# Strassen down-projection of a decoder layer: all 22 row blocks, a third weight buffer, splits moved into the up-projection and parked in HBM

## The chip, the cores and the metric

The kernel runs on one core of one Trainium2 chip. The metric is the device time of one execution in microseconds (us). Before the change three runs took 729.5, 730.12 and 730.3 us; the median is 730.12 us. The profile was taken in a further execution, which took 731.23 us.

## What is computed

One layer of a decoder trunk: a modulated RMSNorm, an input projection into two groups of heads (a gated linear recurrence and sparse attention), an output projection, and then a gated MLP. There are T = 512 tokens and D = 1024 model columns; all arrays are f32. The change lies in the last step, the MLP, cut here to what matters:

```python
h2 = rmsnorm(x, norm2_g[l]) * (1.0 + sc2) + sh2            # 512 x 1024
u = causal_dwconv(h2 @ w_up[l], conv_w[l], conv_b[l])      # 512 x 5632, conv of width 3
a, v = jnp.split(u, 2, axis=-1)
x = x + gt2 * ((jax.nn.silu(a) * v) @ w_down[l])           # (512 x 2816) @ (2816 x 1024)
```

## The kernel before

Matmuls run on fp32r operands. To keep f32 accuracy every operand is held as two fp32r parts: `hi`, a cast of the f32 value on ScalarE (`split`, L140 to L142), and `lo`, the f32 value less `hi`, a subtraction on VectorE. A product of two such operands takes three matmuls (`mm3`, L145 to L147). All work is issued from Python in one fixed order, and each engine runs its own instructions in that order. So an instruction that waits holds up everything behind it on its engine.

**Weights.** `load`, `issue` and `take` (L169, L202, L212) keep two f32 weight tiles, tag `raw`, in SBUF: `take(i)` hands out tile i and issues the load of tile i+1 on SyncE's queue (SP). `parts` splits a tile of 128 x 1024 into `whi` and `wlo`; each of these tags has two buffers. A form, below, is such a pair. The pair that is being consumed by TensorE and the pair that is being made are the two.

**The up stage.** There are 44 steps, two for each of the 22 blocks f of 128 hidden columns (128 rows of `w_down`): step 2f makes the block of `a`, step 2f+1 that of `v`. `up_mm(st)` (L1567) issues the 24 matmuls of a step into one PSUM bank and, ahead of them, the split of the weights of step st+1. `up_post` (L1577), two steps behind, applies the convolution: an ACTIVATE on ScalarE (L1582), two SCALAR_TENSOR_TENSOR on VectorE (L1583, L1584), then for `a` the silu on ScalarE (L1587), for `v` the product with it on GpSimd (L1589). `g_parts` (L1598) then takes the finished block y (128 x 512): it splits what the down stage needs at once, and forms Strassen sums of token halves on GpSimd (L1617 to L1620), which stay in f32. `ada_last` (L1361), one step for each up step as long as it has any (20 of them), computes the vector gt2 on GpSimd from weights that it streams through a tile with tag `aw`.

**The down stage.** The 512 x 2816 by 2816 x 1024 product is done by Strassen's scheme with seven products in place of eight (Winograd's sums), over halves of the tokens, halves of the columns, and pairs of neighbouring row blocks (even, odd). Before, it covers the first 20 of the 22 blocks: ten pairs, taken two at a time in NQ = 5 groups q. The last two blocks are multiplied in the plain way (`plain`, L1794). The four PSUM accumulators, two banks each, are called r, w, s, v. One group of one product is 12 matmuls of 128 x 512 columns: two pairs, two token blocks, three matmuls.

The weight sums are made on the fly: `prep_a` yields the forms b11 and b12-b11, `prep_b` b21 and a sum kept in `keep`, `prep_c` b22 and b22-b12, `prep_d` the two plain blocks and then the kept sums. Each sum is one VectorE TENSOR_TENSOR of 128 x 1024 (L1680, L1685, L1691, L1698). `s_parts` (L1666) splits the f32 token sums `gS` into `gH`, 20 times, between the forms. `ahead_of` (L1743) makes one form ahead of the one in use.

Where Strassen's scheme uses a partial sum in two outputs, the bank is copied out (`taken_snap`, L1732, ScalarE; L1779, VectorE) and folded into the residual rows `rest` on GpSimd (`rest_add`, L1737, with L1740 and L1741), while the bank goes on accumulating. `dn_out` (L1803) multiplies a bank by gt2, adds `rest` (L1806, L1807, VectorE) and stores the result.

SBUF tiles of 4 KB per partition come from one pool, `gran`, of 35 buffers (`G`).

## Time and profile before

| what | value |
|---|---|
| median of three runs | 730.12 us |
| the profiled execution: its time | 731.23 us |
| its span, first to last instruction | 729.1 us |
| mean granted TensorE clock over the span | 0.986 |
| PE busy | 690.1 us, 95% of the span |
| VectorE (DVE) busy | 534.7 us, 73% |
| ScalarE (ACT) busy | 352.7 us, 48% |
| GpSimd (POOL) busy | 190.1 us, 26% |
| moved by DMA | 99.63 MB, 137 GB/s over the span |

The matmuls of the up stage (tile `u`) start between 332.5 and 577.4 us, those of the down stage (tile `dn`) between 580.6 and 725.0 us. Matmuls are pipelined: a row of a 128 x 512 matmul shows about 0.39 us, while the next starts about 0.23 us later. So waits are read from the distance of the starts and from the view of waits, not from the busy time. In the views a row names the engine, the line, the operation, what it writes and reads, and in brackets the idle time of its engine ahead of it with the instruction that ended it. PEclk is the granted TensorE clock, 1.00 being full.

### The profile page before, as it was taken

Reading aid. Unit: us, or ns where it says so; the run is one execution under the profiler, and the core shown is the slowest. Engines: PE = TensorE matmul, PEld = TensorE weight load, DVE = VectorE, ACT = ScalarE, POOL = GpSimd, SP = SyncE. Lnnn points to the kernel's source line nnn. Section 1 sums busy time; section 2 is a strip of 40 time slices with the busy share of each in tenths; the row PEclk is TensorE's granted clock in tenths of the full one; section 3 lists DMA queues with packets and bytes.
Section 4 is the critical chain, followed back from the end, with each engine's and each line's share of the span. In section 5 each row is a group of like instructions: output and inputs, shape, how many; then the busy total and the mean of one; then the engine's idle time right before and its main releaser. Section 6 shows DMA issues by size and latency. Waiting matters only on the chain.

```text
span 729.1 us, 10084 instructions
## 1 busy us (share of the span) xinstructions
PE 690.1 (95%) x3752; PEld 564.2 (77%) x3752; DVE 534.7 (73%) x960; ACT 352.7 (48%) x661; POOL 190.1 (26%) x175
## 2 busy tenths in 40 slices
PE   8999999999999999999999999999999888879857
PEld 4678888688888888889888877788888666658645
DVE  5688989998998986877566656666656557898553
ACT  5554448546777774346433524434343345344311
POOL 1007243330000002000397378332321301230300
PEclk9999999999999999999999999999999989999998
DMA  9997542682321234443535264244243136454220
GB/s 290 284 267 241 174 147 88 195 254 74 116 70 70 69 113 174 118 125 111 157 103 146 82 179 131 72 116 113 65 112 116 58 118 234 167 173 148 83 84 31
DMA packets 101444, 99.63 MB, mean 137 GB/s; under 512 B 5979, under 2 KB 83603, under 8 KB 101397
## 3 DMA queue, kind: packets, MB, share of 16 engines
q1 hardware_dynamic: 100565, 96.80, 43.3%
q10 hardware_dynamic: 832, 2.20, 0.8%
q8 instruction: 29, 0.48, 0.3%
q14 instruction: 18, 0.15, 0.1%
HBM read 94.79 MB, written 4.20 MB: 136 GB/s over the span
## 4 chain that ended last, share of the span: by engine, by line
PE 55%; DVE 24%; ACT 7%; issue 4%; SPq 4%; POOL 3%; DMA 2%; ACTq 0%; POOLq 0%; DVEq 0%
DVE wlo L142 9%; PE u L146 6%; PE u L147 6%; PE u L145 6%; ACT whi L141 4%; PE dn L146 3%; PE dn L147 3%; PE dn L145 3%; PE oT L1050 3%; PE pT L145 2%; PE pT L147 2%; PE pT L146 2%; SPq L282 2%; PE F L1022 2%; DVE y L1584 2%
## 5 line engine op out<-in xcount | busy, mean ns | idle before, releaser
L142 DVE TENSOR_TENSOR wlo<-raw,whi 128x1024 fp32r<-128x1024 f32 (+1 forms) x87 | 118.6, 1364 | 61.2 <-ACT whi L141 60.5
L147 PE MATMUL u<-h2h,wlo 128*128 128x512 f32 (+1 forms) x360 | 137.1, 381 | 1.9 <-DVE wlo L142 1.9
L145 PE MATMUL u<-h2h,whi 128*128 128x512 f32 (+1 forms) x360 | 136.9, 380 | 0.0
L146 PE MATMUL u<-h2l,whi 128*128 128x512 f32 (+1 forms) x360 | 136.8, 380 | 0.0
L141 ACT CAST whi<-raw 128x1024 fp32r<-128x1024 f32 (+1 forms) x87 | 89.5, 1029 | 48.4 <-PE dn L147 24.0
L147 PEld LDWEIGHTS u<-h2h,wlo 128*128 128x128 f32 x360 | 67.7, 188 | 15.9 <-DVE wlo L142 3.2
L146 PEld LDWEIGHTS u<-h2l,whi 128*128 128x128 f32 x360 | 67.7, 188 | 12.8
L145 PEld LDWEIGHTS u<-h2h,whi 128*128 128x128 f32 x360 | 67.7, 188 | 12.7
L1589 POOL TENSOR_TENSOR y<-y,y 128x512 f32<-128x512 f32 x22 | 28.4, 1289 | 130.2 <-DVE y L1584 130.2
L358 POOL TENSOR_TENSOR hrs<-hrs,mhalf 128x4 f32<-128x4 f32 (+2 forms) x16 | 20.1, 1266 | 136.8 <-DVE hrs L357 136.7
L990 ACT ACTIVATE pt<-pt,mx 128x128 f32<-128x128 f32 (+3 forms) x64 | 35.8, 562 | 20.0 <-DVE mx L974 19.7
L1587 ACT ACTIVATE y<-y 128x512 f32<-128x512 f32 x22 | 13.9, 632 | 55.1 <-DVE y L1584 55.1
L141 ACT CAST whi<-keep 128x1024 fp32r<-128x1024 f32 x15 | 15.6, 1049 | 49.8 <-PE dn L147 28.7
L146 PE MATMUL dn<-wlo,gH 128*128 128x512 f32 x80 | 32.7, 409 | 6.9 <-DVE wlo L142 6.9
L145 PE MATMUL pT<-hT,whi 128*128 128x512 f32 x96 | 38.8, 404 | 0.0
L147 PE MATMUL pT<-hT,wlo 128*128 128x512 f32 x96 | 37.6, 392 | 0.0
L146 PE MATMUL pT<-hT,whi 128*128 128x512 f32 x96 | 37.6, 391 | 0.0
L142 DVE TENSOR_TENSOR wlo<-keep,whi 128x1024 fp32r<-128x1024 f32 x15 | 19.0, 1274 | 25.2 <-ACT whi L141 25.1
L146 PE MATMUL dn<-wlo,gT 128*128 128x512 f32 (+1 forms) x58 | 24.6, 425 | 12.5 <-DVE wlo L142 12.5
L1584 DVE SCALAR_TENSOR_TENSOR y<-u,cv,y 128x510 f32<-128x510 f32 x44 | 32.9, 748 | 1.6
L1582 ACT ACTIVATE y<-u,cv 128x512 f32<-128x512 f32 x44 | 33.9, 772 | 0.0
L1583 DVE SCALAR_TENSOR_TENSOR y<-u,cv,y 128x511 f32<-128x511 f32 x44 | 32.6, 741 | 1.4 <-ACT y L1582 1.4
(362 smaller groups left out, 1673.4 us busy)
## 6 DMA issues: line engine op xcount, KB each, us to landing
raw<-in_w_up SPq DMA_DIRECT2D x44, 512.0 KB, 5.2
raw<-in_w_down SPq DMA_DIRECT2D x16, 1024.0 KB, 4.7
aw<-in_w_ada SPq DMA_DIRECT2D x24, 512.0 KB, 4.1
ada<-in_w_ada SPq DMA_DIRECT2D x32, 256.0 KB, 5.8
raw<-in_w_in SPq DMA_DIRECT2D x7, 1024.0 KB, 6.4
x<-in_x SPq DMA_DIRECT2D x8, 512.0 KB, 5.2
raw<-in_w_cmp SPq DMA_DIRECT2D x8, 512.0 KB, 5.1
raw<-in_w_out SPq DMA_DIRECT2D x4, 1024.0 KB, 5.8
```

What stands on the lines that cost most here:

```text
L141: sc.copy(hi, src)
L142: (eng or ve).tensor_tensor(lo, src, f32(hi), ALU.subtract)
L145: pe.matmul(o, ah, bh, start=start, stop=False, skip_group_check=True)
L146: pe.matmul(o, ah, bl, start=False, stop=False, skip_group_check=True)
L147: pe.matmul(o, al, bh, start=False, stop=stop, skip_group_check=True)
L358: gp.tensor_tensor(o, o, mhalf[:, 0:n], ALU.pow)
L990: sc.activation(pt[:, sl], pt[:, sl], AF.Exp, bias=mx[:, e:e + 1], scale=-1.0, accum_out=su[:, h % 2, e:e + 1])
L1050: pe.matmul(oTs[i][r:r + 64, h // 2], VV[:, j, b, g], src[:, q * P:(q + 1) * P], start=(h == 0 and b == 0 and j == 0), stop=False, skip_gr ...
L1582: sc.activation(y, u, AF.Identity, bias=cv[:, 132 + c:133 + c], scale=cv[:, 88 + c:89 + c])
L1583: ve.scalar_tensor_tensor(y[:, 1:], u[:, :T - 1], cv[:, 44 + c:45 + c], y[:, 1:], ALU.mult, ALU.add)
L1584: ve.scalar_tensor_tensor(y[:, 2:], u[:, :T - 2], cv[:, c:c + 1], y[:, 2:], ALU.mult, ALU.add)
L1589: gp.tensor_tensor(ys[0], ys[0], y, ALU.mult)
```

## The change

Six things change, all in the MLP.

1. **All 22 blocks go through Strassen.** NJ becomes 11 pairs, in NQ = 6 groups; the last group has one pair. The plain part goes. The groups are taken in the order SEQ = 0 0 1 1 2 2 3 3 4 5 4 5, the first mention of a group being its first product of a pass, the second its other product. Tiles of half size take their f32 weights from `gran` (`rawd`).
2. **A third weight buffer, two forms ahead.** `form` puts every third form into a tile `w3`, which takes the room of tag `aw` (free once `ada_last` is done). Two calls of `look` ahead of the down stage, and one in each `get`, keep two forms ahead of the one in use. The first two are issued ahead of the last but one `up_post`.
3. **Token sums are split in the up stage.** `g_parts` only notes what is to be split (`pend`); `park`, at the head of the next `up_post`, issues the splits. So the split of the last pair falls into the first pass of the down stage.
4. **Parts that are used late are parked in HBM.** The splits `st22` (256 columns) and `st34` (512) of each pair are written out by ScalarE's queue one `up_post` after that, 22 stores, and read back by SP in the down stage: 11 loads `S34` of 512 KB, 6 loads `A22`, 5 of 512 KB and one of 256 KB.
5. **Banks are seeded instead of folds.** A partial sum that goes into a second output is put into that output's bank, ahead of its products: by ScalarE (`end_a`, bank to bank), by VectorE (`end_b`, `end_c`, with the SBUF copy w5). GpSimd's folds go. Outputs are finished by `dn_out` as their banks complete, two in the third pass and four in the fourth.
6. **`ada_last` takes two steps in every three** (`if st % 3`).

The lines of the changed kernel lie 1 to 6 lines lower in the unchanged parts (L142 becomes L143, L1582 becomes L1588).

```diff
-NJ = 10
-NQ = NJ // 2
+NJ = NFF // 2
+NQ = NJ // 2 + 1
+SEQ = [q for q in range(NQ - 2) for _ in range(2)] + [NQ - 2, NQ - 1] * 2
...
+            if name[0] == "d" and shape[0] * shape[1] <= 1024:
+                raw = G(shape, s="rawd")
+            else:
+                raw = wp.tile([P] + shape, F32, tag="raw", name=nm("raw"))
...
         u = us.pop(st)
+        park()
...
+    def park():
+
+        while parked:
+            sc.dma_start(*parked.pop(0))
+        while pend:
+            split(*pend.pop(0))
+        parked.extend(parking)
+        parking.clear()
...
         if not odd:
-            if b == 0:
-                A1[j // 2] = G([2, 2, 256], F32R, s="gA")
-            split(A1[j // 2][:, b, 0], A1[j // 2][:, b, 1], y[:, h1])
+            gP[j] = G([2, 2, 256], F32R, s="gP")
+            pend.append((gP[j][:, 0, 0], gP[j][:, 0, 1], y[:, h1]))
...
+        pend.extend([(gQ[j][:, 0, 0], gQ[j][:, 0, 1], y[:, h1]), (st22[:, 0], st22[:, 1], y[:, h2]),
+                     (gP[j][:, 1, 0], gP[j][:, 1, 1], s12[:, 0]), (gQ[j][:, 1, 0], gQ[j][:, 1, 1], s12[:, 1]),
+                     (st34[:, 0], st34[:, 1], s34)])
+        parking.extend([(pk22[:, j], f32(st22)), (pk34[:, j], f32(st34))])
...
-        next(ada2, None)
+        if st % 3:
+            next(ada2, None)
...
+    def form(src):
+
+        made[0] += 1
+        if made[0] % 3 != 2:
+            return parts(src)
+        t = wp.tile([P, 2] + list(src.shape)[1:], F32R, tag="aw", name=nm("w3"), bufs=1)
+        split(t[:, 0], t[:, 1], src)
+        return t[:, 0], t[:, 1]
...
     def prep_b(q):
         raw = take(f"db{q}")
-        ve.tensor_tensor(keep[q], raw[:, :, 512:D], keep[q], ALU.subtract)
-        b21 = parts(raw[:, :, 0:512]) if q < NQ - 1 else None
-        if b21:
-            yield b21
-        s_parts(1, q)
-        yield parts(keep[q])
-        ve.tensor_tensor(keep[q], raw[:, :, 0:512], keep[q], ALU.subtract)
-        if not b21:
-            yield parts(raw[:, :, 0:512])
+        b21, b22 = raw[:, :, 0:512], raw[:, :, 512:D]
+        ve.tensor_tensor(keep[q], b22, keep[q], ALU.subtract)
+        yield form(keep[q])
+        yield form(b21)
+        ve.tensor_tensor(keep[q], b21, keep[q], ALU.subtract)
...
+    def phase(xb, x, yb, y, start=False, done=None, each=None):
+        seen = set()
+        for n, q in enumerate(SEQ):
+            w = get()
+            if q not in seen:
+                seen.add(q)
+                product(xb, x, q, w, start)
+                if each:
+                    each(q)
+                if q == NQ - 1:
+                    done()
+            else:
+                product(yb, y, q, w, start)
+
+    def end_a():
+        for a in range(2):
+            sc.copy(bS[a], bR[a])
+
+    def end_b():
+        for a in range(2):
+            ve.tensor_tensor(bV[a], bR[a], w5[a], ALU.add)
...
+    phase(bR, 1, bW, 5, True, end_a, each_a)
+    w5 = [TMP([P, T], tag="w5") for _ in range(2)]
+    for a in range(2):
+        sc.copy(w5[a], bW[a])
+    phase(bR, 6, bS, 2, False, end_b, each_b)
+    phase(bR, 7, bV, 3, False, end_c, each_c)
+    outs = [(bV[0], 0, 1), (bV[1], 1, 1), (bW[0], 2, 1), (bW[1], 3, 1)]
+    ws = []
+    for q in range(NQ):
+        w = get()
+        if q < NQ - 2:
+            product(bR, 4, q, w)
+            dn_out(*outs[q])
+        else:
+            ws += [(hi[:, b], lo[:, b], 2 * q + b) for hi, lo in [w] for b in range(min(2, NJ - 2 * q))]
+    for a, cols in ((0, slice(0, 512)), (1, slice(0, 256)), (1, slice(256, 512))):
+        for n, (hi, lo, j) in enumerate(ws):
+            mm3(bR[a][:, cols], *stat(4, j, a), hi[:, cols], lo[:, cols], False, n == len(ws) - 1)
+        dn_out(bR[a], 2 + a, 0, cols.start, cols.stop)
```

The order of the instructions shows what moved. In the **up stage on ScalarE**, over the four steps of one pair of blocks, before (`gA` and `gT` are the splits of a finished block, `whi` the weights of the next step, `u` a step's PSUM bank):

```order
L1587 ACTIVATE y_5109<-y_5109 128x512
L141 CAST whi_5118<-raw_5041 128x1024
L1582 ACTIVATE y_5146<-u_5040,cv 128x512
L141 CAST gT_5151<-y_5109 128x512
L141 CAST whi_5161<-raw_5041 128x1024
L1582 ACTIVATE y_5189<-u_5080,cv 128x512
L1587 ACTIVATE y_5189<-y_5189 128x512
L141 CAST whi_5198<-raw_5115 128x1024
L1582 ACTIVATE y_5226<-u_5114,cv 128x512
L141 CAST gA_5077<-y_5189 128x256
```

and after the change, the same place in the four steps (`gP`, `gQ` stay in SBUF, the `st` tiles are parked):

```order
L142 CAST whi_5533<-raw_5454 128x1024
L1588 ACTIVATE y_5561<-u_5453,cv 128x512
L142 CAST whi_5576<-raw_5454 128x1024
L142 CAST gQ_5572<-y_5524 128x256
L142 CAST st_997_5573<-y_5524 128x256
L142 CAST gP_5492<-s_994_5566 128x256
L142 CAST gQ_5572<-s_994_5566 128x256
L142 CAST st_998_5574<-s_995_5567 128x512
L1588 ACTIVATE y_5614<-u_5493,cv 128x512
L1593 ACTIVATE y_5614<-y_5614 128x512
L142 CAST whi_5623<-raw_5530 128x1024
L1611 DMA pk_3608<-st_997_5573 128x512
```

The splits now stand behind the next step's `whi`, in one group of five for an odd block, and the two stores follow one step later, in front of the next L1588.

In the **second pass of the down stage on VectorE** (two groups; `keep` the kept weight sum), before:

```order
L1691 TENSOR_TENSOR keep_5696<-raw_5843,keep_5696 128x1024
L1685 TENSOR_TENSOR keep_5747<-raw_5886,keep_5747 128x1024
L142 TENSOR_TENSOR wlo_5943<-raw_5886,whi_5942 128x1024
L142 TENSOR_TENSOR gH_5962<-gS_4510,gH_5962 128x2x256
L142 TENSOR_TENSOR wlo_5966<-keep_5747,whi_5965 128x1024
L1691 TENSOR_TENSOR keep_5747<-raw_5886,keep_5747 128x1024
```

and after (`w` is the third buffer, `wlo` the other two):

```order
L1708 TENSOR_TENSOR keep_5845<-raw_6050,keep_5845 128x1024
L1705 TENSOR_TENSOR keep_5895<-raw_6083,keep_5895 128x1024
L143 TENSOR_TENSOR w_1094_6124<-keep_5895,w_1094_6124 128x1024
L143 TENSOR_TENSOR wlo_6142<-raw_6083,whi_6141 128x1024
L1708 TENSOR_TENSOR keep_5895<-raw_6083,keep_5895 128x1024
```

The `gH` subtraction has gone from between the forms, and the form of the kept sum comes first.

At the **end of the second pass on VectorE**, before:

```order
L1691 TENSOR_TENSOR keep_5864<-raw_6021,keep_5864 128x1024
L142 TENSOR_TENSOR wlo_6084<-raw_6021,whi_6083 128x1024
L1779 TENSOR_TENSOR snap_5905<-dn_5702,snap_5905 128x512
L1779 TENSOR_TENSOR snap_5907<-dn_5706,snap_5907 128x512
L1698 TENSOR_TENSOR raw_6060<-raw_6060 128x2x512
L142 TENSOR_TENSOR gH_6104<-gS_4180,gH_6104 128x2x256
L142 TENSOR_TENSOR wlo_6108<-raw_6060,whi_6107 128x1024
```

and after:

```order
L143 TENSOR_TENSOR wlo_6256<-rawd_6195,whi_6255 128x512
L1798 TENSOR_TENSOR dn_5841<-dn_5835,w_1085_6078 128x512
L1798 TENSOR_TENSOR dn_5842<-dn_5836,w_1086_6079 128x512
L1708 TENSOR_TENSOR keep_6003<-rawd_6195,keep_6003 128x512
L1713 TENSOR_TENSOR raw_6216<-raw_6216 128x2x512
L143 TENSOR_TENSOR wlo_6278<-raw_6216,whi_6277 128x1024
```

The additions L1798 read the first accumulator and write into another bank, and the sum and the form that open the third pass stand behind them.

More of the change, by code (lines that the diff above doesn't have):

```diff
@@ L1698, in prep_c @@
         ve.tensor_tensor(b12, b22, b12, ALU.subtract)
[L1699 to L1720 removed]
+        yield form(b12)
@@ new lines, in prep_c, with forms, load_s34 @@
+        yield form(b22)
+    def forms():
+        for prep_ in (prep_a, prep_b, prep_c):
+            gens = [prep_(q) for q in range(NQ)]
+            for n, q in enumerate(SEQ):
+                yield next(gens[q])
+                if q in SEQ[:n]:
+                    next(gens[q], None)
+        for q in range(NQ):
+            yield form(keep[q])
+    def load_s34(j):
+        if j < NJ:
+            S34[j] = G([2, 2, 256], F32R, s="S34")
+            sp.dma_start(f32(S34[j]), pk34[:, j])
@@ new lines, in load_a22, with load_rest, stat @@
+    def load_a22(q):
+        n = min(2, NJ - 2 * q)
+        A22[q] = G([n, 2, 256], F32R, s="A22")
+        sp.dma_start(f32(A22[q]), pk22[:, 2 * q:2 * q + n])
+    def load_rest():
+        rest.append(G([D], s="rest"))
+        sp.dma_start(rest[-1], x1d[:, len(rest) - 1])
+    def stat(n, j, a):
+        sl = slice(a * P, a * P + P)
+        t = {1: lambda: gP[j][:, 0], 5: lambda: gP[j][:, 1], 2: lambda: gQ[j][:, 0], 6: lambda: gQ[j][:, 1],
+             7: lambda: S34[j][:, :, 0], 3: lambda: S34[j][:, :, 1], 4: lambda: A22[j // 2][:, j % 2]}[n]()
@@ L1721, in stat, with product @@
         return t[:, 0, sl], t[:, 1, sl]
-    def product(o, n, q, w, first, last=False):
+    def product(bank, n, q, w, start=False):
         hi, lo = w
-        for b in range(2):
-            for tp_ in range(2):
-                if (o, tp_) not in bank:
-                    bank[o, tp_] = PS("dn")
-                mm3(bank[o, tp_], *stat(n, 2 * q + b, tp_), hi[:, b], lo[:, b], first and q == 0 and b == 0, False)
-    def taken_snap(o, tp_):
-        t = TMP([P, T], tag="snap")
-        sc.copy(t, bank[o, tp_])
-        return t
@@ L1737, in rest_add @@
-    def rest_add(tp_, row, col, t):
-        i, cols = 2 * row + tp_, slice(512 * col, 512 * col + 512)
-        gp.tensor_tensor(t, t, gt2[:, cols], ALU.mult)
-        gp.tensor_tensor(rest[i][:, cols], rest[i][:, cols], t, ALU.add)
-    def ahead_of(gen):
-        held = [next(gen)]
-        def get():
-            w = held.pop()
-            nxt = next(gen, None)
-            if nxt is not None:
-                held.append(nxt)
-            return w
-        return get
-    up_post(nst - 2)
@@ L1756, in hybrid_layer_kernel @@
-    get = ahead_of(chain(*[prep_a(q) for q in range(NQ)], *[prep_b(q) for q in range(NQ)],
-                         *[prep_c(q) for q in range(NQ)], prep_d()))
-    rest = []
-    for q in range(NQ):
-        product("r", "a11", q, get(), True)
-        if q == 0:
-            up_post(nst - 1)
-        if q == NQ - 1:
-            s1 = [taken_snap("r", a) for a in range(2)]
-        product("w", 0, q, get(), True)
-    w5 = [taken_snap("w", a) for a in range(2)]
-    for i in range(NT):
-        rest.append(G([D], s="rest"))
-        sp.dma_start(rest[i], x1d[:, i])
@@ L1791, in hybrid_layer_kernel @@
-    for a in range(2):
-        rest_add(a, 1, 1, s3[a])
-    def plain(o, tp_, b, w, last):
-        hi, lo = w
-        i, half = {"s": (tp_, 0), "v": (tp_, 1), "r": (2 + tp_, 0), "w": (2 + tp_, 1)}[o]
-        g = A2[2 * NJ + b]
-        sl, cols = slice(i * P, i * P + P), slice(512 * half, 512 * half + 512)
-        mm3(bank[o, tp_], g[:, 0, sl], g[:, 1, sl], hi[:, 0, cols], lo[:, 0, cols], False, last)
-        if last:
-            dn_out(bank[o, tp_], i, half, 0, 512)
-    def dn_out(acc, i, half, c0, c1):
+        for b in range(min(2, NJ - 2 * q)):
+            for a in range(2):
+                mm3(bank[a], *stat(n, 2 * q + b, a), hi[:, b], lo[:, b], start and q + b == 0, False)
@@ L1804, in dn_out, with look, get @@
+    ready = []
+    source = forms()
+    def look():
+        w = next(source, None)
+        if w is not None:
+            ready.append(w)
+    def get():
+        look()
+        return ready.pop(0)
+    def dn_out(acc, i, half, c0=0, c1=512):
         cols = slice(half * 512 + c0, half * 512 + c1)
```

150 lines of the change are left out of this document (57 added, 93 removed).

## Prediction

> **What bounds the kernel now.** I began with the busy time by stretches, asking of each stage whether TensorE waits. The columns are the stretch, its length, the busy time and count on PE, PEld, DVE, ACT and POOL, the granted clock, the DMA share and GB/s.
>
> ```profile
> 520.00:577.40 57.40, 57.40 (x255) 47.54 (x254) 33.47 (x39) 22.67 (x31) 19.95 (x18) 1.00 0.32 94
> 577.40:725.80 148.40, 121.14 (x476) 93.15 (x474) 104.46 (x102) 53.84 (x66) 23.24 (x13) 0.93 0.37 126
> ```
>
> At its end the up stage is full: TensorE works at full clock without a hole. The down stage is not, and nearly all that the change can win lies there. How much it is, the order of time on PE says. Four of its rows: a matmul of the up stage's last step, the last one of that step, the first matmul of half width at the end, and the sixth of these.
>
> ```profile
> 574.71 0.39 PE L147 MATMUL u<-h2h,wlo 128*128 128x512 f32 x1
> 577.43 0.39 PE L147 MATMUL u<-h2h,wlo 128*128 128x512 f32 x1
> 722.31 0.28 PE L145 MATMUL dn<-whi,gT 128*128 128x256 f32 x1
> 722.90 0.28 PE L147 MATMUL dn<-whi,gT 128*128 128x256 f32 x1
> ```
>
> The first two starts are twelve matmuls apart: 2.72 / 12 = 0.227 us for a full one. The last two are five apart: 0.118 us for one of half width. By the code the down stage has 420 matmuls of Strassen products and 48 plain ones, of which six are cut into twelve halves; so 462 full ones stand between 577.43 + 0.23 = 577.66 and 722.31. They need 462 x 0.227 = 104.9 us and took 144.6. **39.7 us are lost.** The view of waits in this window names most of it (total us, times, longest), and the rows of PE at two places show the two ways in which it is lost; the stretches around the first place stand behind them.
>
> ```profile
> ACT whi L141 <- PE dn L147: 52.7, 19, 11.9
> PE dn L146 <- DVE wlo L142: 20.9, 15, 6.5
> PE dn L145 <- ACT whi L141: 4.7, 3, 2.8
> 590.45 0.49 PE L145 MATMUL dn<-whi,gA 128*128 128x512 f32 x1 [1.49 <-ACT whi L141]
> 591.70 0.50 PE L146 MATMUL dn<-wlo,gA 128*128 128x512 f32 x1 [0.76 <-DVE wlo L142]
> 588.00:592.60 4.60, 2.35 (x10) 1.41 (x9) 2.87 (x4) 2.09 (x3) 0.80 (x1) 1.00 0.00 0
> 592.60:596.00 3.40, 3.40 (x10) 2.60 (x9) 2.02 (x2) 1.05 (x1) 0.00 (x0) 0.50 0.44 128
> 686.88 0.50 PE L146 MATMUL dn<-wlo,gT 128*128 128x512 f32 x1 [0.87 <-DVE wlo L142]
> 689.10 0.50 PE L146 MATMUL dn<-wlo,gT 128*128 128x512 f32 x1 [1.26 <-DVE wlo L142]
> ```
>
> TensorE waits for weight forms, and ScalarE, which begins each form, waits for TensorE to give a buffer back: two buffers chase each other. And after a stretch in which half of 4.6 us was idle, the clock is granted at 0.50 for 3.4 us. A mean clock of 0.93 over 148.4 us is 148.4 x 0.07 = 10.4 us lost; the other 29.3 us are waits.
>
> **The matmuls.** Strassen on 11 pairs is 11 x 42 = 462 matmuls, nine of them now cut in two: 453 full ones, 102.8 us, where it was 104.9. The tail gains three halves in its last run, +0.35 us; the three more in the run ahead lie beside the `dn_out` that runs then.
>
> **The weight forms with three buffers.** This is the main term. Rows of VectorE and ScalarE with GpSimd quiet, among them one form that hangs on a sum, and one row beside a fold of GpSimd's:
>
> ```profile
> 636.57 1.22 DVE L1691 TENSOR_TENSOR keep<-raw,keep 128x1024 f32<-128x1024 f32 x1
> 637.71 1.22 DVE L1685 TENSOR_TENSOR keep<-raw,keep 128x1024 f32<-128x1024 f32 x1
> 598.92 1.22 DVE L1680 TENSOR_TENSOR keep<-raw 128x1024 f32<-128x1024 f32 x1
> 600.25 1.05 ACT L141 CAST whi<-keep 128x1024 fp32r<-128x1024 f32 x1 [2.59 <-DVE keep L1680]
> 601.33 1.23 DVE L142 TENSOR_TENSOR wlo<-keep,whi 128x1024 fp32r<-128x1024 f32 x1 [1.19 <-ACT whi L141]
> 621.69 2.20 DVE L1691 TENSOR_TENSOR keep<-raw,keep 128x1024 f32<-128x1024 f32 x1
> 622.88 2.14 POOL L1741 TENSOR_TENSOR rest<-rest,snap 128x512 f32<-128x512 f32 x1
> L142 DVE TENSOR_TENSOR gH<-gS,gH 128x512 fp32r<-128x512 f32 x20 | 15.8, 792 | 0.7 <-ACT gH L141 0.7
> L1807 DVE TENSOR_TENSOR tmp<-tmp,rest 128x512 f32<-128x512 f32 x7 | 4.8, 692 | 0.7
> ```
>
> Independent operations of 128 x 1024 start 637.71 - 636.57 = 1.14 us apart. A form whose sum stands right ahead of it takes 601.33 - 598.92 = 2.41 us from the sum's start to that of its subtraction, as VectorE idles through ScalarE's cast. A `dn_out` is two operations like L1807, 1.4 us. TensorE takes 12 x 0.227 = 2.72 us for a form, 5.45 for a group's two. With the 15.8 us of `gH` gone, VectorE needs for a group:
>
> - first pass: sum, form, form, 3 x 1.14 = 3.4 us (the second form's cast hides behind the first form), under 5.45;
> - second pass: sum to subtraction 2.41, then that form, the other form and the kept sum 3 x 1.14, together 5.8 us, over by 0.4;
> - third pass: 2.41 + 2 x 1.14 = 4.7 us, and 6.1 in the two groups with a `dn_out`, which the lead gained in the others covers;
> - fourth: one form and one `dn_out`, 2.5 us against 2.72.
>
> So only the second pass falls behind: 0.4 us in each of four full groups and, as halves keep whole delays, about 0.7 in the last two together, some 2.3. A form that is ready ahead covers about 1 of it; I put **1.3 us**. The bounds are 0 (all covered) and 4 (four kept sums beside GpSimd, each 2.20 - 1.22 = 1.0 longer as at 621.69). What made those rows slow goes: the folds, after which GpSimd has only the last pair's work.
>
> **The start.** TensorE's first wait of the stage was this, for a cast that stood behind the work of step 42:
>
> ```profile
> 580.58 0.50 PE L145 MATMUL dn<-whi,gA 128*128 128x512 f32 x1 [2.76 <-ACT whi L141]
> 573.79 0.75 DVE L1584 SCALAR_TENSOR_TENSOR y<-u,cv,y 128x510 f32<-128x510 f32 x1
> ```
>
> Now the first two forms stand ahead of it. The cast needs a buffer of step 42, free at 577.66 - 5.45 = 572.2; VectorE is done with step 41 at 574.5, and a sum and a subtraction later, 574.5 + 2 x 1.2 = 576.9, the form is ready, before TensorE asks at 577.66. Cost nothing; with step 41 later than before, at worst 2.
>
> **Seeds.** Their prices, from operations of the same kind and size:
>
> ```profile
> L1734 ACT COPY snap<-dn 128x512 f32<-128x512 f32 x6 | 3.4, 586 | 3.4 <-PE dn L147 3.2
> L1779 DVE TENSOR_TENSOR snap<-dn,snap 128x512 f32<-128x512 f32 x2 | 1.3, 684 | 0.0
> ```
>
> When a pass's last product into R ends, 18 matmuls (4.1 us) into the other bank remain. First pass: two copies 1.2, cast 1.05, subtraction 1.23, all inside 4.1. Third: two additions 1.3 and a subtraction, inside. Second: VectorE, which by then has no lead, ends its last half form about 0.9 us after R, comes to the additions (L1798), and behind them are queued a half kept sum 0.6 and `prep_c`'s first sum and form: 0.9 + 1.3 + 0.6 + 2.41 + 1.14 = 6.4 against 4.1. **A stall of 2.3 us** opens the third pass; bounds 1 (VectorE in time for R) and 4. No row shows a bank written from a bank; I take the price of bank to SBUF, and bound it by half and by double, 0.6 us either way, inside these bounds.
>
> **The clock.** A stall of 2.3 us in two parts is like 1.49 + 0.76 at 590, which halved the clock, and like 0.87 + 1.26 at 687, which did not. A chance of 0.4 on 3.4 / 2 = 1.7 us: 0.7 us. The Trainium skill, page "TensorE: Matmul & The Clock Gate", section "HAM oscillation — how this bites in real kernels", asks only that no idle gap of TensorE exceed some 3.4 us; by it this term is zero and the sum 0.7 less. The trace disagrees: ahead of 592.6 no single wait was over 1.49 us.
>
> **The up stage.** ScalarE's rows show how little TensorE's pace has to spare:
>
> ```profile
> 539.55 1.05 ACT L141 CAST whi<-raw 128x1024 fp32r<-128x1024 f32 x1 [0.58 <-PE u L146]
> 544.77 0.62 ACT L141 CAST gT<-y 128x512 fp32r<-128x512 f32 x1 [3.49 <-POOL y L1589]
> 566.53 0.62 ACT L141 CAST gT<-y 128x512 fp32r<-128x512 f32 x1 [3.49 <-POOL y L1589]
> 513.01 0.41 ACT L141 CAST gA<-y 128x256 fp32r<-128x256 f32 x1 [3.52 <-POOL y L1589]
> PE u L147 <- DVE wlo L142: 1.9, 3, 1.3
> 315.45 0.63 ACT L1466 ACTIVATE sq<-x 128x512 f32<-128x512 f32 x1 [1.98 <-DVE x L1464]
> 315.46 0.36 ACTq L1634 DMA_DIRECT2D x1d<-x  x1
> ```
>
> A pair of blocks takes 566.53 - 544.77 = 21.76 us, of which ScalarE's in-order chain of casts and waits fills all but 0.6. The change adds three casts a pair, 2 x 0.41 + 0.62 = 1.4 us, and two stores of 0.36, and once a pair ScalarE waits for the last of GpSimd's sums, with the next L1588 queued behind. It takes away the two waits of 3.5 us, since a `whi` now runs ahead of the splits while GpSimd multiplies. I reckon the chain to come out about as long as it was, plus a little of the stores. Bounds: -1.9 (the 1.9 us above go) to +13: 1.4 + 0.7 - 0.6 = 1.5 us a pair over 11 pairs is 16.5, less the 5.45 - 1.05 - 1.23 = 3.2 us that ScalarE may fall behind before TensorE waits. I take **+1.5**, nearer to the lower end, as the last casts stood in time that the chain now frees.
>
> **DMA.** The parked parts add 5.8 + 2.9 MB of loads; some 30 MB cross in the down stage.
>
> ```profile
> raw<-in_w_down SPq DMA_DIRECT2D x14, 1024.0 KB, 4.7
> rest<-x1d SPq DMA_DIRECT2D x4, 512.0 KB, 7.4
> GB/s 0 6 268 0 124 150 220 103 230 151 351 320 136 138 272 2 272 87 194 271 3 40 235 140 142 266 217 61 0 0 0 0 0 206 195 10 0 0 103 34
> ```
>
> The second pass is worst: 5.5 weight tiles, seven `S34` and two `rest`, 10.5 MB in 30 us, 350 GB/s, as much as the best slice of the down stage above. But `S34` is wanted a pass later, and most of it is queued on SP behind the weight tile of the moment. A weight tile is held 5.8 us, and its successor must land in the 5.8 us in which the other tile is worked on; 4.7 fits. Cost nothing. If each landed as late as `rest`, which queued behind others, a group takes (5.8 + 7.4) / 2 = 6.6, 0.8 more, over the 11 groups of two passes some 8 us. The Trainium skill, "DMA: Bandwidth & Descriptors", section "Specifications", gives a core about 358 GB/s of HBM; by that the second pass would stand at 98% of the limit, which speaks against this change. The trace's 351 is one slice of 3.8 us, and no run here holds such a rate for long.
>
> **The sum**, against the profiled execution: 577.66 + 1.5 + 102.8 + 1.3 + 2.3 + 0.7 + 0.5 (an estimate for waits under 0.3 us) = 686.8; then, as before, from the first half matmul to the execution's end 731.23 - 722.31 = 8.9, and 0.35: 696.0. The median of the runs is 1.1 us under the profiled execution: **695 us**.
>
> **Rivals.**
>
> - *DMA sets the pace* of the second and third pass: +8, 703 us. For it the 350 GB/s, against it the landing after 4.7. Chance 0.10.
> - *ScalarE's chain sets the up stage's pace*: +13 in place of +1.5, 706 us. For it the spare 0.6 us. Chance 0.12.
> - *The third buffer does not do what it says*: VectorE's in-order stream, not the buffers, made the forms late. Half of the 39.7 stays in place of my 4.8: +15, 710 us. Against it the 52.7 us for which ScalarE waited on TensorE. Chance 0.04.
> - *Slower*: a store on ScalarE's queue holds ScalarE until its data have landed, for `x1d` 3.1 us (row below). Two a pair put 6.2 on a chain with 0.6 to spare, 11 x 5.6 = 60 us, more than the 35 won: 755 us. It decides from about 3.8 us a pair. The rows at 315.45 speak against it: ScalarE starts while its queue issues. Chance 0.04.
>
> ```profile
> x1d<-x ACTq DMA_DIRECT2D x4, 512.0 KB, 3.1
> ```
>
> **Numbers.** The forecast keeps 0.70. Its own range is 687 (up stage -1.9, no waits, no half clock) to 702 (the upper bounds of start, second pass, stall and clock). To hold the rivals at 703 and 706 the range is 687 to 707. A measurement of this kernel can tell about 0.2% (1.5 us) from no change; faster 0.95, same 0.01, slower 0.04.
>
> **What would show it.** Right: the up stage's last matmul starts at 576 to 581; the down stage has a clock near 1.00; TensorE's longest wait there is some 2 us, at the opening of the third pass, for `wlo` behind L1798; GpSimd is idle after the last pair. Wrong: `u` matmuls that wait for `wlo` all along, `raw` landing after 6 us or more with VectorE's sums waiting for DMA, or half-clock stretches in the second pass.

## The result and the profile after

| | before | after |
|---|---|---|
| median of the runs (lowest to highest), us | 730.21 (729.5 to 730.95) | 707.2 (706.83 to 709.98) |
| profiled execution, us | 731.23 | 707.41 |
| its span, us | 729.1 | 705.6 |
| TensorE's mean granted clock | 0.986 | 0.993 |

The ratio is 0.9693, with a 95% interval of 0.9666 to 0.9719: 23 us faster, where the prediction had 35. The direction was right. The time lies 12 us above the forecast and 0.2 us outside the range.

The stretches of the changed kernel, in the same columns as in the prediction (length, busy time and count on PE, PEld, DVE, ACT, POOL, granted clock, DMA share, GB/s). The first two are the second half of the up stage, the other three the first three passes of the down stage.

```profile
460.00:520.00 60.00, 56.46 (x244) 45.15 (x244) 42.23 (x49) 27.34 (x43) 37.18 (x30) 1.00 0.50 149
520.00:583.50 63.50, 63.19 (x277) 51.46 (x275) 43.13 (x52) 30.33 (x48) 20.93 (x18) 1.00 0.42 132
583.50:619.90 36.40, 32.39 (x132) 26.23 (x132) 32.15 (x32) 18.36 (x25) 10.82 (x6) 0.91 0.66 247
619.90:651.40 31.50, 31.16 (x133) 24.46 (x132) 25.52 (x25) 10.39 (x13) 0.00 (x0) 1.00 0.79 298
651.40:685.40 34.00, 32.09 (x134) 25.90 (x133) 23.82 (x25) 13.60 (x14) 0.00 (x0) 0.95 0.79 273
```

The second pass is full (31.16 of 31.50 us busy), and the 60 us from 460 hold 244 matmuls at full clock, where 60 / 0.227 = 264 fit. So TensorE now waits in a stage where it hardly waited before. The order of time on PE gives the edges: the last matmul of the up stage, the first two of the down stage, the two that open the third pass, the first half matmul at the end.

```profile
583.28 0.39 PE L148 MATMUL u<-h2h,wlo 128*128 128x512 f32 x1
584.20 0.51 PE L146 MATMUL dn<-whi,gP 128*128 128x512 f32 x1 [0.54 <-ACT whi L142]
588.18 0.79 PE L147 MATMUL dn<-wlo,gP 128*128 128x512 f32 x1 [3.47 <-DVE wlo L143]
652.95 0.51 PE L146 MATMUL dn<-whi,S 128*128 128x512 f32 x1 [1.16 <-ACT whi L142]
654.21 0.79 PE L147 MATMUL dn<-wlo,S 128*128 128x512 f32 x1 [0.75 <-DVE wlo L143]
698.50 0.28 PE L146 MATMUL dn<-w,A 128*128 128x256 f32 x1
```

After both of these openings the clock was halved:

```profile
588.20:592.60 4.40, 4.40 (x10) 3.45 (x11) 3.94 (x5) 1.46 (x2) 0.00 (x0) 0.50 0.70 238
654.20:657.40 3.20, 3.19 (x8) 2.52 (x9) 2.32 (x2) 0.00 (x0) 0.00 (x0) 0.50 0.32 45
```

From these rows the sum can be made again. The up stage ends at 583.28 + 0.23 = 583.51. From there to 698.50 are 115.0 us for 102.8 us of full matmuls: 12.2 us are lost, where before 39.7 were. I took each interval between two starts on PE, less 0.227 us, and put it to the wait, the half clock or the pass in which it lies (0.1 us goes in rounding):

| term | forecast, us | measured, us |
|---|---|---|
| up stage, against 577.66 | +1.5 | +5.9 |
| start of the down stage | 0, at worst 2 | 4.4 |
| second pass, VectorE | 1.3 | 1.5 |
| opening of the third pass | 2.3 | 2.3 |
| half clock | 0.7 | 3.7 (2.1 and 1.6) |
| small waits | 0.5 | 0.2 |
| from the first half matmul to the end | 9.25 | 8.9 |

The gain itself is there: the wait that bounded the down stage before, 52.7 us of ScalarE for a buffer, is now this (total us, times, longest, in the down stage), and a weight tile lands almost as fast as before (5.0 us from issue to landing, where it was 4.7).

```profile
ACT whi L142 <- PE dn L148: 16.3, 11, 4.8
raw<-in_w_down SPq DMA_DIRECT2D x15, 1024.0 KB, 5.0
```

What is missing went in the up stage and at the opening that follows it. The waits of ScalarE between 340 and 583 us show what its splits wait for:

```profile
ACT y L1593 <- DVE y L1590: 37.4, 20, 3.7
ACT gP L142 <- POOL y L1595: 29.9, 9, 3.6
ACT gP L142 <- POOL s L1628: 15.4, 9, 1.8
ACT gQ L142 <- POOL y L1595: 7.8, 8, 3.5
ACT gQ L142 <- POOL s L1629: 5.2, 10, 1.0
ACT st L142 <- POOL s L1630: 4.7, 10, 0.5
```

In a pair of blocks that is 3.3 + 1.7 + 1.0 + 0.5 + 0.5 = 7.0 us of waiting for GpSimd, as much as the two waits of 3.5 us that I had taken away. One cast of each pair, the last that hangs on a sum, shows the pace: its first row, and the last two.

```profile
370.60 0.62 ACT L142 CAST st<-s 128x512 fp32r<-128x512 f32 x1 [0.47 <-POOL s L1630]
556.18 0.62 ACT L142 CAST st<-s 128x512 fp32r<-128x512 f32 x1 [0.47 <-POOL s L1630]
578.54 0.62 ACT L142 CAST st<-s 128x512 fp32r<-128x512 f32 x1 [0.48 <-POOL s L1630]
```

The last two are 22.4 us apart, where GpSimd has nothing else to do; on average it is (578.54 - 370.60) / 9 = 23.1 us. TensorE needs 21.76. So this chain falls behind TensorE, by 1.3 us a pair on average and 0.6 in the last. Where its lead is used up TensorE waits (3.5 us between 460 and 520). From 520 on TensorE loses only 0.3 us, while the chain goes on falling behind and runs late into the down stage. At the boundary ScalarE, VectorE and GpSimd did this:

```profile
583.12 1.03 ACT L142 CAST whi<-raw 128x1024 fp32r<-128x1024 f32 x1
```

```profile
584.04 0.75 DVE L1590 SCALAR_TENSOR_TENSOR y<-u,cv,y 128x510 f32<-128x510 f32 x1
584.70 1.21 DVE L1698 TENSOR_TENSOR keep<-raw 128x1024 f32<-128x1024 f32 x1
585.84 2.29 DVE L143 TENSOR_TENSOR wlo<-raw,whi 128x1024 fp32r<-128x1024 f32 x1
```

```profile
584.93 2.11 POOL L1595 TENSOR_TENSOR y<-y,y 128x512 f32<-128x512 f32 x1 [6.42 <-DVE y L1590]
```

The first form's cast came behind step 41's Identity at 582.44, its subtraction behind step 41's shifted additions and the first sum. VectorE was to be done with step 41 at 574.5, 3.2 us ahead of TensorE's end; it was done at 584.8, 1.3 us after it. GpSimd's product of that step then ran beside the subtraction, which took 2.29 us in place of 1.22.

### The profile page after: what moved, and what is told of

It is laid out like the page before. It is cut to its first block, busy times and chain, and to the rows that moved or that the text cites. A ratio compares the mean times of both kernels' runs of the same rounds, so it can differ in the third digit from the quotient of the medians.

```text
span 705.6 us, 10223 instructions
## 1 busy us (share of the span) xinstructions
PE 682.9 (97%) x3749; PEld 559.8 (79%) x3749; DVE 547.1 (78%) x995; ACT 360.0 (51%) x688; POOL 181.7 (26%) x167
## 5 line engine op out<-in xcount | busy, mean ns | idle before, releaser
L143 DVE TENSOR_TENSOR wlo<-raw,whi 128x1024 fp32r<-128x1024 f32 (+1 forms) x77 | 101.0, 1313 | 61.0 <-ACT whi L142 57.4
L142 ACT CAST whi<-raw 128x1024 fp32r<-128x1024 f32 (+1 forms) x77 | 78.9, 1025 | 57.9 <-PE u L147 26.4
L1595 POOL TENSOR_TENSOR y<-y,y 128x512 f32<-128x512 f32 x22 | 38.1, 1733 | 132.8 <-DVE y L1590 103.0
L1588 ACT ACTIVATE y<-u,cv 128x512 f32<-128x512 f32 x44 | 34.1, 774 | 0.3 <-PE u L148 0.3
L1034 ACT COPY pT<-F 128x512 f32<-128x512 f32 (+2 forms) x52 | 25.9, 499 | 13.7 <-PE F L1027 13.3
L979 DVE CUSTOM_DVE_ANT_0 pt<-S,cmask 128x128 f32<-128x128 f32 (+3 forms) x64 | 29.7, 485 | 3.3 <-PE S L974 3.3
L1304 DVE SCALAR_TENSOR_TENSOR aacc<-aw,cs,aacc 128x1024 f32<-128x1024 f32 x21 | 28.8, 1370 | 0.0
L1027 PE MATMUL F<-cb,pt 128*128 128x128 f32 x160 | 25.6, 274 | 1.1 <-ACT pt L995 1.0
```

What stands on the lines that cost most here:

```text
L142: sc.copy(hi, src)
L143: (eng or ve).tensor_tensor(lo, src, f32(hi), ALU.subtract)
L979: ve.tensor_tensor_reduce(pt[:, sl], ps[:, sl], cmask[:, 512 - W:512], -1.0, 1e30, ALU.add, ALU.min, mx[:, e:e + 1])
L1304: ve.scalar_tensor_tensor(o, w, cs[:, k:k + 1], o, ALU.mult, ALU.add)
L1588: sc.activation(y, u, AF.Identity, bias=cv[:, 132 + c:133 + c], scale=cv[:, 88 + c:89 + c])
L1595: gp.tensor_tensor(ys[0], ys[0], y, ALU.mult)
```

## The experiments

Theory A: in the up stage the splits stand in the in-order queues of ScalarE and VectorE ahead of the next block's chain, and wait there for GpSimd. Rivals: B, the added casts and subtractions are themselves too much work; C, the thinned cadence of `ada_last`; D, the stores on ScalarE's queue. In all experiments times are medians of 4 or 5 runs beside runs of the kernel before on the same chip; the ratios are to that kernel.

**e1_cadence**: `ada_last` takes a step every time again.

```diff
-        if st % 3:
-            next(ada2, None)
+        next(ada2, None)
```

> One part of the change undone: ada_last takes a step in every step of the up stage again, not in two of three. Theory A (the up stage runs late because ScalarE, in order, waits in each pair of blocks for GpSimd's product and sums, 3.4 + 0.6 + 2.8 us, so that its chain takes 23.1 us a pair where TensorE takes 21.8): the waits stay, the last u matmul starts at 582 to 584 (583.3 after the change), time 705 to 708. Theory C (the thinned cadence, which spreads GpSimd's ada_last work over the stretch 460 to 520): the last u matmul starts at 578 to 580, time 702 to 704.

709.58 us, ratio 0.9712 (0.9695 to 0.9730). The last `u` matmul started at 585.36, 2.1 us later than in the changed kernel. Theory C falls. The end is later than theory A's 582 to 584 too, and the time above what both expected; that the thinner cadence helps a little isn't shown, since the intervals of the two ratios overlap, and the half clock behind the start lasted longer here (5.8 us at 0.51).

**e2_store_sp**: the stores go through SP's queue.

```diff
-            sc.dma_start(*parked.pop(0))
+            sp.dma_start(*parked.pop(0))
```

> The parked parts are stored by SP's queue in place of ScalarE's. Theory D (the stores hold ScalarE; two a pair with a wait each): the chain of a pair gets over 1 us shorter and the last u matmul starts at 577 to 579, time 700 to 703. Theory A: ScalarE does not wait for what its queue issues, the last u matmul starts at 582.5 to 584, time 706 to 709 (later rather than earlier, as SP now waits for the split ahead of its next raw load).

708.32 us, ratio 0.9693 (0.9673 to 0.9714), the last `u` matmul at 583.86, both as theory A expected. Theory D falls, and with it the mechanism of the prediction's rival of 755 us. A row of the changed kernel shows why: while two stores are issued, ScalarE has Silu running and starts a cast.

```profile
491.36 0.63 ACT L1593 ACTIVATE y<-y 128x512 f32<-128x512 f32 x1 [1.93 <-DVE y L1590]
491.46 0.81 ACTq L1611 DMA_DIRECT2D pk<-st  x2
491.89 1.04 ACT L142 CAST whi<-raw 128x1024 fp32r<-128x1024 f32 x1
```

**e4_no_sum_wait**: the same casts and subtractions, but the three splits of sums read the block itself. The sums are made and not used, so the kernel leaves out the products of sums and its numbers differ.

```diff
-  (gP[j][:, 1, 0], gP[j][:, 1, 1], s12[:, 0]), (gQ[j][:, 1, 0], gQ[j][:, 1, 1], s12[:, 1]),
-  (st34[:, 0], st34[:, 1], s34)])
+  (gP[j][:, 1, 0], gP[j][:, 1, 1], y[:, h1]), (gQ[j][:, 1, 0], gQ[j][:, 1, 1], y[:, h2]),
+  (st34[:, 0], st34[:, 1], y.rearrange("p (a b) -> p a b", a=2))])
```

> As many splits of the same shapes, stores and sums as after the change, but the three splits of the sums take the block itself as their source, so that they do not wait for GpSimd's sums (the products of those sums are left out: other numbers are multiplied). Theory A: 2.8 us of waits a pair go, the product's 3.4 + 0.6 stay; 23.1 - 2.8 = 20.3 us is under TensorE's 21.8, so the last u matmul starts at 577.5 to 579.5 and the time is 697 to 702. Theory B (the added casts and subtractions themselves): 582 to 584 and 705 to 708.

707.4 us, ratio 0.9678 (0.9649 to 0.9708), and the last `u` matmul at 585.35, some 3.0 us of it from a stretch of 6.1 us at a clock of 0.50 behind 471.5; without that it would be about 582.4 (an estimate: 585.35 less 3.0), where theory B had it. The waits for the sums were gone and hardly anything was won: theory A, as I had put it, missed. The waiting had moved: ScalarE's wait for VectorE ahead of Silu rose from 37.4 us to this, and its waits for VectorE and GpSimd in this window came to 100 us as before (100.4, now 100.0). One such place reads so on ScalarE and VectorE:

```profile
ACT y L1593 <- DVE y L1590: 64.9, 20, 6.2
```

```profile
488.94 1.26 DVE L143 TENSOR_TENSOR gP<-y,gP 128x256 fp32r<-128x256 f32 x1
490.12 1.50 DVE L143 TENSOR_TENSOR gQ<-y,gQ 128x256 fp32r<-128x256 f32 x1
491.55 1.52 DVE L143 TENSOR_TENSOR st<-y,st 128x512 fp32r<-128x512 f32 x1
493.00 0.74 DVE L1589 SCALAR_TENSOR_TENSOR y<-u,cv,y 128x511 f32<-128x511 f32 x1
```

```profile
494.62 0.63 ACT L1593 ACTIVATE y<-y 128x512 f32<-128x512 f32 x1 [6.18 <-DVE y L1590]
```

The five subtractions stand ahead of the next block's shifted additions on VectorE, and beside GpSimd's work a subtraction of 128x256 takes up to 1.50 us (0.41 alone, in a row of e10 below). The product's waits (28.3 and 6.8 us) were still there as well, so e4 takes away only a part of theory A's waits. Theory A had to be widened: not the wait for one engine, but the place of the splits ahead of the chain on both. The next two kernels test that place and leave all work in.

**e3_late_park**: the splits are issued behind the product of the odd step, a step or more later.

```diff
         u = us.pop(st)
-        park()
...
             gp.tensor_tensor(ys[0], ys[0], y, ALU.mult)
+            park()
```

> The same splits and stores, but issued a step or more later: behind the product of the odd step, so that GpSimd is long done when ScalarE comes to them. Nothing is left out. Theory A: ScalarE's waits for GpSimd (3.4 + 0.6 + 2.8 us a pair) go, a pair takes TensorE's 21.8 us, the last u matmul starts at 577 to 579, the first wlo of the down stage comes 3 to 5 us earlier against the end of the up stage, and the time is 695 to 700. Theory B (the added casts and subtractions are themselves too much for ScalarE and VectorE): the last u matmul starts at 582 to 584, time 705 to 708.

695.3 us, ratio 0.9519 (0.9499 to 0.9540); repeated as **e3_again** 695.52, ratio 0.9523 (0.9502 to 0.9543). The last `u` matmul starts at 574.80, earlier than the 577 to 579 of theory A; the start of the down stage waits 0.8 us, and no half clock follows it:

```profile
574.80 0.39 PE L148 MATMUL u<-h2h,wlo 128*128 128x512 f32 x1
576.20 0.50 PE L147 MATMUL dn<-wlo,gP 128*128 128x512 f32 x1 [0.79 <-DVE wlo L143]
```

Theory B falls: the same casts, subtractions and stores fit. Up stage, start and the first half clock have one cause. A long wait alone is no sign of it: here ScalarE still waits 61.3 us for VectorE ahead of Silu, 20 times, 6.2 us at the longest, almost as in e4, and TensorE waits 0.3 us in the whole stage; what is gone is all waiting of the splits for GpSimd.

> The kernel of e3_late_park once more, for a comparison on the same chip as e9_flip: 694 to 696.5 us, the third pass's opening at 2.3 us.

**e10_mid_park**: on the changed kernel, the splits stay in their step and only move behind that step's Identity and shifted additions.

```diff
         u = us.pop(st)
-        park()
...
         ve.scalar_tensor_tensor(y[:, 2:], u[:, :T - 2], ...)
+        park()
         ys[s] = y
```

> The changed kernel with the splits in the same step as after the change, but behind that step's Identity and its two shifted additions instead of ahead of them. GpSimd has some 1 to 3 us more, not a whole step. If what counts is that the splits stand ahead of the next block's chain in the queues of ScalarE and VectorE, this repairs most: last u matmul at 575 to 579, time 697 to 701. If the splits must be a whole step late, since ScalarE still waits in order for the product (3.4 us) and the sums, the last u matmul starts at 580 to 584, time 702 to 708.

693.12 us, ratio 0.9484 (0.9457 to 0.9510), faster than either theory had it, and no kernel here was faster. The window of the up stage has no idle PE left (234.60 busy of 234.60 us), and the down stage follows without a wait; the row behind is of VectorE, a split with GpSimd quiet.

```profile
340.00:574.60 234.60, 234.60 (x1080) 196.13 (x1079) 160.08 (x197) 114.29 (x179) 111.72 (x95) 1.00 0.49 146
```

```profile
574.63 0.39 PE L148 MATMUL u<-h2h,wlo 128*128 128x512 f32 x1
574.85 0.39 PE L146 MATMUL dn<-whi,gP 128*128 128x512 f32 x1
```

```profile
525.32 0.41 DVE L143 TENSOR_TENSOR gP<-s,gP 128x256 fp32r<-128x256 f32 x1
```

So the splits needn't be a whole step late: one Identity and two additions ahead of them, some 2.3 us, are enough. Their place is the cause of the 5.9, the 4.4 and 2.1 of the 3.7 us. In the up stage, up to 575, the move did two things at once. The waits of the splits for GpSimd fell from 63.0 us (the five lines above, up to 583) to 12.0, and the one ahead of Silu from 37.4 to 16.6. ScalarE now waits for TensorE instead, as an engine does that has a lead; in the changed kernel this line had 26.4 us:

```profile
ACT whi L142 <- PE u L147: 80.7, 35, 3.7
```

No run takes away one of the two alone, so how the 14 us divide between the waits for GpSimd and VectorE's order is not shown.

**e5_two_buffers** and **e6_one_ahead** stand on e3_late_park and take the two parts of the main term away, one each.

```diff
-        if made[0] % 3 != 2:
-            return parts(src)
-        t = wp.tile([P, 2] + list(src.shape)[1:], F32R, tag="aw", name=nm("w3"), bufs=1)
-        split(t[:, 0], t[:, 1], src)
-        return t[:, 0], t[:, 1]
+        return parts(src)
```

> On top of e3_late_park (695.3 us; down stage from 575.0 to the first half matmul at 686.8, 111.8 us for 102.8 us of full matmuls), the third weight buffer of the down stage is taken away: each form uses the two buffers in turn, still two forms ahead in order. Theory of the prediction (the third buffer carries the gain in the down stage, since with two a form's 1.05 + 1.23 us can start only when TensorE begins the form before, and VectorE's sums and seeds then have no slack): the down stage gets 8 to 15 us longer, first and second pass above all, time 703 to 710. Rival (VectorE's in-order stream made the forms late, and the folds' going is the gain): under 3 us, time 695 to 698.

```diff
-    look()
     look()
     up_post(nst - 2)
```

> On top of e3_late_park, three buffers, but forms are issued one ahead instead of two. If it is the buffers that count, the order of issue alone costs little: 0 to 2 us, time 695 to 697. If the forms must stand two ahead in VectorE's and ScalarE's queues (ahead of the seeds and of the last two steps' work), the start and each opening of a pass wait longer, 3 to 8 us, time 698 to 703.

With two buffers: 705.58 us, ratio 0.9670 (0.9651 to 0.9690), 10.3 us more than e3_late_park. ScalarE's wait for a buffer and TensorE's for a form grew from the first pair of lines (e3_late_park, down stage) to the second (e5).

```profile
ACT whi L142 <- PE dn L148: 13.7, 8, 4.8
PE dn L147 <- DVE wlo L143: 2.8, 4, 1.0
```

```profile
ACT whi L142 <- PE dn L148: 42.2, 28, 3.6
PE dn L147 <- DVE wlo L143: 9.8, 16, 1.0
```

The third buffer counts, and the rival of under 3 us falls. But it is not the whole gain. From the end of the up stage (575.50 + 0.23) to the first half matmul (696.34) e5 takes 120.6 us for 102.8 us of full matmuls, so it loses 17.8; e3_late_park, from 575.03 to 686.02 (not the 686.8 of the expectation), loses 8.2, and the kernel before lost 39.7. Some 22 us of the gain stay without the third buffer. They come from what else changed (the order two ahead, the folds and the `gH` splits gone), and no run takes the last two away.

One form ahead in place of two: 703.77 us, ratio 0.9639 (0.9614 to 0.9664), 8.5 us more, a little above what its second theory expected. That theory is right in kind: with three buffers, a form still comes late if it stands behind the last steps' chains in the queues. The longest of its waits is at the third form of the stage. The sum ahead of that form ran beside GpSimd and took 2.31 us, and two stretches of 3.4 and 3.5 us at a clock of 0.51, behind this wait and behind the opening of the third pass, are part of the profiled execution's time.

```profile
585.78 0.50 PE L147 MATMUL dn<-wlo,gP 128*128 128x512 f32 x1 [2.64 <-DVE wlo L143]
```

**e7_scalar_seeds** (on e3_late_park) takes the additions at the end of the second and third pass off VectorE.

```diff
-            ve.tensor_tensor(bV[a], bR[a], w5[a], ALU.add)
+            sc.copy(bV[a], bR[a])
...
         sc.copy(w5[a], bW[a])
+        gp.tensor_tensor(w5[a], w5[a], gt2[:, 512:D], ALU.mult)
...
         sp.dma_start(rest[-1], x1d[:, len(rest) - 1])
+        gp.tensor_tensor(rest[-1][:, 512:D], rest[-1][:, 512:D], w5[(len(rest) - 1) % 2], ALU.add)
```

(`bW` in the third pass in the same way.)

> On top of e3_late_park, the additions on VectorE at the end of the second and third pass become copies on ScalarE, and the summand w5 goes into the residual instead, by GpSimd (2 products and 4 additions, which it does beside the second to fourth pass). The prediction's step says that the third pass opens late since VectorE, with no lead, has the 1.3 us of additions ahead of the pass's first sum: then the opening's 2.3 us (waits 1.2 + 0.8) shrink by 1.2 to 1.3 us, and the time is 693.5 to 695, less if GpSimd slows VectorE by up to 1 us an operation. If a late raw tile or TensorE's return of a buffer sets the opening, it stays at 2.3 and the time is 695 to 697.

697.41 us, ratio 0.9555 (0.9536 to 0.9574): slower than e3_late_park and than either theory had it. The step itself was right, since the third pass now opened with one wait of 0.76 us where there had been 1.20 + 0.77. But what this won was lost again one group later (0.76 us at 650.16), where VectorE had waited 2.07 us for a weight tile. And GpSimd's two products fell on the opening of the second pass, where VectorE has no lead either, and a new wait of 1.24 us stands there, with one of 0.77 behind it (GpSimd, VectorE, PE):

```profile
608.76 4.08 POOL L1832 TENSOR_TENSOR w<-w,gt 128x512 f32<-128x512 f32 x2 [17.22 <-ACT w L1831]
```

```profile
609.38 2.31 DVE L1708 TENSOR_TENSOR keep<-raw,keep 128x1024 f32<-128x1024 f32 x1
```

```profile
615.11 0.49 PE L146 MATMUL dn<-whi,gQ 128*128 128x512 f32 x1 [1.24 <-ACT whi L142]
```

**e8_best** adds two changes of order to e7: the first form ahead of the first sum at the start, and the order of e9 below.

```diff
+        w = form(b11) if q == 0 else None
         ve.tensor_tensor(keep[q], b12, b11, ALU.subtract)
-        yield form(b11)
+        yield w or form(b11)
```

> e7_scalar_seeds, and two changes of order: at the start the form of the block itself stands ahead of the first sum, and the third pass opens with the product whose weight form needs no sum. By the theory (VectorE's order sets both openings) the start's wait of 0.8 us for wlo goes and the third pass opens with under 0.6 us of waits: 691.5 to 693.5 us. If the openings hang on something else, 694 to 696.

698.97 us, ratio 0.9577 (0.9559 to 0.9595), above both expectations. The start's first wait (0.79 us) went, and later forms of the first pass waited in its place, 0.4, 0.3 and 0.8 us, ahead of the wait of 1.0 that e7 has too. Behind the opening of the second pass the clock stood at 0.51 for 3.5 us, which it didn't in e7. Here an engine that is behind loses the same work somewhere, whatever stands first.

**e9_flip** (on e3_late_park): the third pass opens with the form that needs no sum.

```diff
+        if q == 0:
+            yield form(b22)
         ve.tensor_tensor(b12, b22, b12, ALU.subtract)
         yield form(b12)
-        yield form(b22)
+        if q:
+            yield form(b22)
...
-            if q not in seen:
-                seen.add(q)
+            first = q not in seen
+            seen.add(q)
+            if first != (flip and q == 0):
```

> On top of e3_late_park, only the order of the first two products of the third pass is changed: it opens with the product whose weight form needs no sum (b22), so that the additions on VectorE are followed by that form's subtraction and the sum and form of the other product come while TensorE works. By VectorE's rows of e3_late_park the subtraction ends 0.1 us after the second pass, the next one 0.5 us late: the third pass's opening loses 0.3 to 1.0 us instead of 2.3, time 693.5 to 694.5. If a buffer, or the raw tile, sets the opening: 695 to 696.

695.78 us, ratio 0.9523 (0.9499 to 0.9546): no gain. The first product opened on time, and the next two forms were late instead, the second of them by this wait. The VectorE row shows what stood behind it: the sum of the next weight tile waited for that tile.

```profile
647.67 0.50 PE L147 MATMUL dn<-wlo,S 128*128 128x512 f32 x1 [0.76 <-DVE wlo L143]
```

```profile
643.92 1.23 DVE L1715 TENSOR_TENSOR raw<-raw 128x1024 f32<-128x1024 f32 x1 [0.68 <-DMA raw<-in_w_down]
```

**e11_rest_later**: e10_mid_park with the order of e9_flip, and 1 MB of `rest` loaded in the third pass instead of at the end of the second.

```diff
-        if q > 3:
-            load_rest()
...
-        if q in (1, 2):
-            dn_out(bS[q - 1], q - 1, 0)
+        if q == 0:
+            load_rest()
+            load_rest()
+        if q in (2, 3):
+            dn_out(bS[q - 2], q - 2, 0)
```

> e10_mid_park with the order of e9_flip at the opening of the third pass, and with the first two loads of the residual (1 MB) moved out of the end of the second pass into the third. In e9_flip the second stall of the opening (0.3 + 0.8 us at 646) followed a raw weight tile that landed 7.7 us after its issue, while the DMA engines stood at 417 GB/s; VectorE waited 0.7 us for it. If the transfers queued ahead of that tile made it late, it lands 1 to 2.5 us earlier, the second stall goes, the opening costs under 1.2 us instead of 2.3, and the time is 690.5 to 692.3. If VectorE's backlog alone sets the opening, the stall only moves again: 692.5 to 694.

693.12 us, ratio 0.9495 (0.9474 to 0.9515), the same as e10. The opening lost 1.5 us in place of 2.3, but 1.3 us were lost again later in the pass, behind a tile that now had `rest` ahead of it on SP's queue (that this made it late is not tested):

```profile
652.66 1.23 DVE L1715 TENSOR_TENSOR raw<-raw 128x1024 f32<-128x1024 f32 x1 [2.13 <-DMA raw<-in_w_down]
```

What the third pass could gain beyond e10 stays open: VectorE's backlog and the transfers stand close behind each other there, and no run moved both.

## Why the prediction was wrong

- **The up stage: the step that failed.** The prediction put the chain of ScalarE at its old length: "It takes away the two waits of 3.5 us, since a `whi` now runs ahead of the splits while GpSimd multiplies. I reckon the chain to come out about as long as it was." The `whi` does run ahead, but it is the short part: ScalarE still stood 3.3 us of each pair before the product and 3.7 before the sums and the second product, and the new subtractions took VectorE's time ahead of the next block's additions. The bounds (-1.9 to +13) held the 5.9; the choice of the lower end had no row behind it. Of the signs it named, the last `u` matmul came at 583.28 instead of 576 to 581, and the longest wait, 3.47 us, stood at the start instead of at the third pass. With only the place of the splits changed, the stage ends at 574.86 (e10), 2.8 us before that of the kernel before.
- **The start: failed with it.** I priced step 41 at its old place and allowed 2 us for a later one. A chain that is 1.3 us a pair too slow piles up over nine pairs, and what TensorE has not yet lost of it falls due where the next stage needs the same engines. The rival "ScalarE's chain" (0.12, 706 us) had about the right sum: its 13 us came as 5.9 in the up stage, 4.4 at the start and 2.1 of half clock behind it. Its mechanism was in part right: in the changed kernel and in e4 VectorE's queue holds up the chain as well. That the time came within 0.2 us of the range is luck: the range was widened to 707 for rivals, and its own sum let the up stage or the start be late, not both.
- **The clock: right in kind, too small.** One half-clock stretch at odds of 0.4 was expected, at the third pass; two came, the other behind the start. Two of its readings of the kernel before are off, and no term of the sum rests on them: the 10.4 us lost by the clock are some 9 in the rows (the mean also counts 6.6 us from 704.0, at 0.85, in which TensorE was idle but for 0.15), and ahead of 592.6 there was also a wait of 2.76 us, at 580.58, with a half clock of its own. The rule of the Trainium skill ("TensorE: Matmul & The Clock Gate", section "HAM oscillation — how this bites in real kernels": no idle gap over some 3.4 us) gives none for the opening of the third pass, whose waits were 1.16 and 0.75; the trace shows 0.50 behind them. Behind the start's 3.47 rule and trace agree.
- **The third buffer, two forms ahead: right in sum, shown in part.** Of 39.7 us lost in the down stage 12.2 were left, and 8.2 in e3_late_park; 52.7 us of waiting for buffers became 16.3. Taking the buffer away costs 10.3 us, the order 8.5 (both on e3). That two buffers chasing each other made the whole loss isn't shown: with two buffers, in e5, more than half of it was gone.
- **Second pass 1.3 and third opening 2.3: right**, at 1.5 and 2.3. That the additions are part of the opening, e7 shows.
- **DMA at nothing: right for this kernel.** Tiles land in 5.0 us and the second pass is full. It moved 298 GB/s on average where 350 were forecast, but 390 over its last 11.4 us (640.0 to 651.4), with TensorE busy for 11.32 of them; in e9 13 us ran at 397 (628 to 641). The figure of about 358 GB/s that the Trainium skill gives a core ("DMA: Bandwidth & Descriptors", section "Specifications") was no limit in these traces. At the opening of the third pass the landing of tiles is next in line (e7, e9, e11).
- **The seeds: right.** The unseen copy from bank to bank took 0.57 us, the addition into a bank 0.69.
- **The stores: right.** They hold nobody (e2).
- **GpSimd idle after the last pair: right.** There is no POOL work between 619.9 and 685.4.

## What to carry to other kernels

Work that waits for a slow engine is better put behind the next item's chain in every in-order queue it enters than ahead of it: here that was one line moved, worth 14 us. A stage with 0.6 us to spare in a pair is to be costed as a cycle (who waits for whom, once round, on each engine), and its overrun is due at the next stage's start as well. Where an engine is behind, changing what it does first moves the stall and does not remove it.
